# A norm moved between the weight pieces of a product, its factor in another buffer, and one attention unit held behind the query norms

## The chip, the core and the metric

The kernel runs on one core of a Trainium2 chip. The metric is the device time of one execution in microseconds (us); lower is better. The core has five engines that run side by side, each with its own queue of instructions in a fixed order: TensorE (PE in the profile, with its weight loads as PEld), VectorE (DVE), ScalarE (ACT), GpSimd (POOL) and SyncE (SP), which here issues most of the transfers.

## What is computed

One layer of a streaming encoder over 320 frames (256 of a prompt, 64 of a running stream), 2048 channels wide, all in float32:

```python
z = rmsnorm(x, ln_g) @ w_in                 # 1024 q, 128 k, 128 v, 1024 u, 1024 gate columns
q, k = rmsnorm(q, q_g), rmsnorm(k, k_g)     # per head of 64
attn_o = sink_attention(q, k_band, v_band, bias, sinks)
u, sv = gelu(zs)[..., :1024], rmsnorm(gelu(zs)[..., 1024:], g)
sgu_o = u * (ws @ sv + b_s)
mix = concatenate([rmsnorm(attn_o, g_a), rmsnorm(sgu_o, g_s)])
x = x + mix @ w_out
x = x + square(relu(rmsnorm(x, ln_ffn) @ w_up)) @ w_down
```

The norm of the attention output, `rmsnorm(attn_o, g_a)`, is the one that the change moves. As a norm's factor is one number per frame, the kernel multiplies by it behind the product: `g_a` goes into the left operand, the factor `rm_a` into the eviction of the W_out products.

## The kernel before

**Products.** Every large product is done by `products` (L115). It takes 256 output columns at a time and walks the contraction in weight pieces of 4 x 128 rows. Each piece is loaded by SP (`w_raw`, L103), split into a high and a low part (`w_hi` on ACT, L108; `w_lo` on DVE, L109), and multiplied with the high and low parts of the activations in 24 matmuls (L133). A product over 2048 channels has four pieces, 96 matmuls; a W_out product is one half of the contraction, two pieces, 48 matmuls. `w_hi` and `w_lo` have three buffers each, the accumulators in PSUM two. SP's loads are put in a fixed order by `issue_after` in `load`.

**Order.** A scheduler places each engine's instructions by a simulated timeline; it prefers what stands earlier in the program and pulls later work forward while that cannot run. Two tools hold it: `tc.issue_after(ins)` puts what is traced in its block behind `ins` on the same engine, and `between_pieces` of `products` puts a small piece of work behind weight piece number n of a product. In the second case the rest of the product stands behind `narrow[-1]`, the last matmul that the small work has recorded in the list `narrow`. Before the change, `rstd` (L163), `norm_q` (L306) and `values` (L318) record theirs there; `rstd_rows` (L152) and `spread` (L184) do not.

**First stage.** The first stage computes, in this order: keys, values and the first quarter of the queries; three more query products (q1 to q3), with the norms of earlier ones between their pieces; four gate products ("v", L465), among which ten attention units are spread (`attend_next` takes 4, 3, 3 and 0 units ahead of the four); four u products (L498); then 16 W_out products (L530), and the two MLP products. `norm_q(2)` stands behind piece 0 of q3; `norm_q(3)` behind q3.

**Attention units.** Unit n is one block of 64 frames and one of two key heads. Its score matmuls (L383) go into one PSUM tile `s_ps` (one buffer), DVE adds the bias with the query's norm `rq` (L392), maxima, exponentials (ACT, L407) and the division by the sum (POOL, L411) follow, then transposes (L421), their copy (L423), the product with the values (L427) and the copy into `ao` (L430).

**The norm of the attention output.** `add_square` sums the squares of `ao` in `acc_a` during u products 0 to 2 (POOL, L439). `rstd_rows` then takes the mean over the channels with six matmul instructions (three matmuls, L156, each of which the profile shows as two), an add on DVE (L158) and a power of -0.5 on POOL (L160); `spread` brings the result across all partitions with three more matmuls (L188, six in the profile) and copies it to `rm_a` (DVE, L190). Before, both stand behind the whole of the last u product (L511 to L513). `rm_a` is first used in the eviction of the first W_out product (L533).

**Memory.** `acc_a`, the bias, the gate's weights `wsT` and the gate's bias `sgb` lie in the pool `at`, which is closed behind the u products (L522). The pool `wf`, seven buffers for the weight pieces of W_out and of the MLP, is opened right behind it (L523) in the space that became free. The factors `rx`, `rk`, `rm_a`, `rm_s` and `r2` take turns in two buffers (`rstd_b`, L193); `rx` is read until the GELU of the last u product, `rk` until the keys are done.

Of the kernel before, what the change touches and what calls it, by code (L numbers as in the profile page):

```python
# [15 lines left out]
P = 128  # L16
# [4 lines left out]
KT = DM // P  # L21
DFF = 8192
FB = 16
EPS = 1e-6
# [6 lines left out]
def hymba_step_kernel(ctx: ExitStack, tc: tile.TileContext, i, o):  # L31
    nc = tc.nc
# [12 lines left out]
    def misc():  # L45
        return ps_m.tile([P, 512], F32, name="misc", tag="misc")
# [4 lines left out]
    def blk(name, shape, dt=F32):  # L51
        return actp.tile(shape, dt, name=name, tag="B", bufs=6)
# [15 lines left out]
    ident = const.tile([P, P], F32, name="ident")  # L68
# [10 lines left out]
    inv_1k = const.tile([P, 1], F32, name="inv_1k")  # L79
# [16 lines left out]
    loads, between, steps, narrow = [], [], [], []  # L96
# [18 lines left out]
    def products(w, k0, nk, c0, ps, rh, rl, deep=None, between_pieces={}):  # L115

        wv = w.rearrange("(kt p) n -> p kt n", p=P)
        behind = None  # L120
        steps.clear()
        for a in range(0, nk, 4):
            raw = (deep or wp).tile([P, 4, 256], F32, name="w_raw", tag="w_raw")
            hi, lo = w_tiles()
            load(raw, wv[:, k0 + a:k0 + a + 4, c0:c0 + 256])
            high, low = halves(raw, hi, lo)
            tail = isinstance(ps, list) and a + 4 == nk
            for k, g in [(k, g) for g in range(2) for k in range(4)] if tail else [(k, g) for k in range(4) for g in range(2)]:
                kk = a + k
                for x, (w_, r_) in enumerate(((hi, rh), (hi, rl), (lo, rh))):  # L130
                    out = ps[g][:, 0:T] if isinstance(ps, list) else ps[:, g, 0:T]
                    with tc.issue_after(behind) if behind else nullcontext():
                        mm = nc.tensor.matmul(out=out, lhsT=w_[:, k, g * P:(g + 1) * P], rhs=r_(kk),  # L133
                                              start=(kk == 0 and x == 0), stop=(kk == nk - 1 and x == 2))
            steps.append((high, low, mm.ins))
            if a // 4 in between_pieces:
                with tc.issue_after(mm.ins):
                    between_pieces[a // 4]()
                    behind = narrow[-1]

    def sums(name):
        return sm.tile([P, T], F32, name=name, tag="ssq", bufs=2)

    def acc_tile():
        return ps_acc.tile([P, 2, 512], F32, name="acc", tag="acc")

    def product(w, k0, nk, c0, rh, rl, deep=None, apart=False, **kw):
        ps = [misc(), misc()] if apart else acc_tile()
        products(w, k0, nk, c0, ps, rh, rl, deep=deep, **kw)
        return ps  # L150

    def rstd_rows(sq, weight, eps):  # L152

        st = misc()
        for t in range(3):
            nc.tensor.matmul(out=st[:, t:t + 1], lhsT=sq[:, t * P:(t + 1) * P], rhs=weight, start=True, stop=True)  # L156
        r = sm.tile([P, 3], F32, name="r_rows", tag="r_rows")
        nc.vector.tensor_scalar(out=r, in0=st[:, 0:3], scalar1=eps, scalar2=None, op0=ALU.add)  # L158
        rs = sm.tile([P, 3], F32, name="rs_rows", tag="rs_rows")
        nc.gpsimd.tensor_tensor(out=rs, in0=r, in1=nhalf[:, 0:3], op=ALU.pow)  # L160
        return rs
# [22 lines left out]
    def spread(rs, out):  # L184

        bc = misc()
        for t, (t0, n) in enumerate(TT):
            nc.tensor.matmul(out=bc[:, t0:t0 + n], lhsT=rs[:, t:t + 1].to_broadcast([P, P]),  # L188
                             rhs=ident[:, 0:n], start=True, stop=True)
        nc.vector.tensor_copy(out=out, in_=bc[:, 0:T])  # L190
        return out

    def rstd_b(name):  # L193
        return sm.tile([P, T], F32, name=name, tag="rstd_b", bufs=2)

    def split(src, g, hi, lo, pinned=False):

        pin = tc.keep_in_program_order if pinned else lambda ins: ins
        pin(nc.scalar.activation(out=hi, in_=src, func=AF.Copy, scale=g))
        pin(nc.vector.scalar_tensor_tensor(out=lo, in0=src, scalar=g, in1=hi.bitcast(F32), op0=ALU.mult,  # L200
                                           op1=ALU.subtract))
# [3 lines left out]
    xh, xl = (lambda k: XH[:, k]), (lambda k: XL[:, k])  # L205
    w_in = i["w_in"]
# [8 lines left out]
    for a, n in [(a, 1) for a in range(8)] + [(a, 2) for a in range(8, KT, 2)]:  # L215
# [16 lines left out]
        for x, (w_, r_) in enumerate(((hi, xh), (hi, xl), (lo, xh))):  # L232
            for j, k, g in [(j, k, g) for j in range(2) for k in range(n) for g in range(2)]:
                ps = q0_ps if j == 0 else kv_ps
                mm = nc.tensor.matmul(out=ps[:, g, 0:T], lhsT=w_[:, j, k, g * P:(g + 1) * P], rhs=r_(a + k),  # L235
                                      start=(a + k == 0 and x == 0), stop=(a + k == KT - 1 and x == 2))
# [46 lines left out]
    for k in range(0, KT, 2):  # L283
        sq = sm.tile([P, 2, T], F32, name="sq2", tag="w2", bufs=4) if k else ssq2
# [4 lines left out]
    ssq = sums("ssq")  # L289
    nc.vector.tensor_tensor(out=ssq, in0=ssq2[:, 0], in1=ssq2[:, 1], op=ALU.add)  # L290

    rx, rk = rstd_b("rx"), rstd_b("rk")

    rq = at.tile([P, 4, 10], F32, name="rq", bufs=1)

# [10 lines left out]
    def norm_q(g, sq):  # L306
        st = misc()
        for b in range(5):
            mm = nc.tensor.matmul(out=st[:, 2 * b:2 * b + 2], lhsT=sq[:, b].rearrange("p a t -> p (a t)"), rhs=hone,  # L309
                                  start=True, stop=True)  # L310
        narrow.append(mm.ins)
        r = at.tile([P, 10], F32, name="r_q", tag="r_q")
        nc.vector.tensor_scalar(out=r, in0=st[:, 0:10], scalar1=HD * EPS, scalar2=None, op0=ALU.add)
        nc.gpsimd.tensor_tensor(out=rq[:, g], in0=r, in1=nhalf[:, 0:10], op=ALU.pow)
# [26 lines left out]
    def keys():  # L341
        for dst, c in ((kn[:, 0:256], slice(0, 256)), (kn[:, 384:448], slice(256, 320))):
            nc.vector.scalar_tensor_tensor(out=dst, in0=zk[:, c], scalar=g_k, in1=rk[:, c], op0=ALU.mult, op1=ALU.mult)
        for h in range(2):
# [11 lines left out]
                    between_pieces={0: first_norms, 1: lambda: norm_q(1, q1_sq[0]), 2: keys})  # L356
# [76 lines left out]
    def add_square(acc, src, first):  # L433
        if first:
            nc.scalar.activation(out=acc[:, 0:T], in_=src, func=AF.Square)
        else:
            sq = sm.tile([P, T], F32, name="sq", tag="w1", bufs=3)
            nc.scalar.activation(out=sq, in_=src, func=AF.Square)
            nc.gpsimd.tensor_tensor(out=acc[:, 0:T], in0=acc[:, 0:T], in1=sq, op=ALU.add)  # L439

    todo = list(range(10))

    def attend_next(n):
        for _ in range(n):
            attend(todo.pop(0))


    def gelu2(ps, out):
# [10 lines left out]
    def sums_rows(name):  # L459
        t = at.tile([P, TP], F32, name=name, tag="ssq_rows", bufs=1)  # L460
        nc.gpsimd.memset(t[:, T:TP], 0.0)
        return t

    acc_v = sums_rows("acc_v")
    for g in range(4):  # L465
# [3 lines left out]
        for a in range(2 * g, 2 * g + 2):  # L469
            add_square(acc_v, gv[:, a], a == 0)  # L470
            nc.gpsimd.tensor_scalar(out=gv[:, a], in0=gv[:, a], scalar1=g_sv[:, a:a + 1], scalar2=None, op0=ALU.mult)
    nc.gpsimd.memset(wsT[HD:P, :, 0:HD], 0.0)
    rv = rstd_rows(acc_v, inv_1k, 4 * EPS)
    vnat = blk("vnat", [P, 2, 1024])
    vnat_s = at.tile([P, 1024], F32, name="vnat_s", bufs=1)
# [18 lines left out]
        nc.vector.tensor_tensor(out=gv[:, g, 256:T], in0=sp_ps[:, 256:T], in1=sgb[:, g, 0:HD], op=ALU.add)  # L494

    acc_s = sums("acc_s")
    SH = SL = None
    for g in range(4):  # L498
        u_ps = product(w_in, 0, KT, 1280 + g * 256, xh, xl)
        if g == 0:  # L500
            acc_a = sums_rows("acc_a")
            AH, AL = blk("AH", [P, 8, T], F32R), blk("AL", [P, 8, T], F32R)
            SH, SL = blk("SH", [P, 8, T], F32R), blk("SL", [P, 8, T], F32R)
        for x in range(2):
            a, (high, low, _) = 2 * g + x, steps[2 * x + 1]
            with tc.issue_after(high), tc.issue_after(low):
                split(ao[:, a], g_oa[:, a:a + 1], AH[:, a], AL[:, a])
        for x, a in enumerate(range(3 * g, min(3 * g + 3, 8))):
            with tc.issue_after(steps[x][0]):
                add_square(acc_a, ao[:, a], a == 0)  # L510
        if g == 3:  # L511
            with tc.issue_after(steps[0][0]), tc.issue_after(steps[0][1]):
                rm_a = spread(rstd_rows(acc_a, inv_1k, EPS), rstd_b("rm_a"))  # L513
        gu = sm.tile([P, 2, T], F32, name="gu", tag="w2", bufs=4)
        gelu2(u_ps, gu)
        sp = gv[:, 2 * g:2 * g + 2]
        nc.vector.scalar_tensor_tensor(out=sp, in0=sp, scalar=0.5, in1=gu, op0=ALU.mult, op1=ALU.mult)
        for a in range(2 * g, 2 * g + 2):
            add_square(acc_s, gv[:, a], a == 0)
            split(gv[:, a], g_os[:, a:a + 1], SH[:, a], SL[:, a])  # L520

# [6 lines left out]
    rm_s = rstd_b("rm_s")  # L528
    for half, (hi, lo, rm) in enumerate(((AH, AL, rm_a), (SH, SL, rm_s))):
        for g in range(8):  # L530
            ps = product(i["w_out"], 8 * half, 8, g * 256, lambda k: hi[:, k], lambda k: lo[:, k], wf)
            t = sm.tile([P, 2, T], F32, name="to", tag="w2", bufs=4)
# [15 lines left out]
    for b in range(nb):  # L548
        FH = [blk(f"FH{h}", [P, 8, T], F32R) for h in range(2)]
        FL = [blk(f"FL{h}", [P, 8, T], F32R) for h in range(2)]  # L550
        for g in range(FB // 2):
            ps = product(i["w_up"], 0, KT, (b * FB + 2 * g) * P, hh_, hl_, wf)
            t = sm.tile([P, 2, T], F32, name="tf", tag="w2", bufs=4)
# [83 lines left out]
```

## Time and profile before

| | |
|---|---|
| median of 3 timed runs | 1266.09 us (1265.51 to 1266.98) |
| the profiled execution: its time | 1261.78 us |
| its span, first to last instruction | 1259.8 us |
| mean granted clock of TensorE | 0.997 |
| DMA, mean over the span | 149 GB/s, 187.78 MB |
| HBM read / written | 182.91 MB / 3.32 MB |

A page of the profile gives busy times of the engines, the span in 40 slices, the DMA queues, the chain of work that ended last, and the costliest groups of instructions. Other views list who waited for whom, the busy time of each engine in a window, and the instructions in order of time. In the timeline a row has start, duration, engine, line of the code, operation, tiles as output<-inputs, shapes and count; a bracket at its end gives the idle time of the engine just ahead and what ended it. Matmuls overlap, so the distance between two starts, not the duration of one, is the pace. A trailing q in an engine's name (SPq) means its instruction queue. The columns of a window are length, busy time and instructions of PE, PEld, DVE, ACT and POOL, then the clock that TensorE was granted (1.00 is full), the share of the DMA engines, and GB/s.

### The profile page before, as it was taken

The page shows a single profiled execution, that of the slowest core. Times are in us where ns is not written, and L with a number is a line of the kernel's source. Part 1 is how long each engine was busy: PE and PEld are TensorE (multiplying, and loading weights), DVE is VectorE, ACT ScalarE, POOL GpSimd, SP SyncE. Part 2 cuts the span into 40 slices and gives each one's busy share as a digit, 9 for nine tenths or more (in the row PEclk, how much of TensorE's full clock was granted, in tenths as well). Part 3 has the DMA queues.
Part 4 walks back from the last instruction along what each step waited for, and adds up shares of the span by engine and source line. Part 5 has one row for each costly group of instructions (what it writes and reads, how often), then busy time and mean ns, then how long its engine had stood idle before and what let it go on. Part 6 is the DMA issues. An engine that isn't in the chain of part 4 may idle for free.

```text
span 1259.8 us, 20220 instructions
## 1 busy us (share of the span) xinstructions
PE 1248.1 (99%) x8519; PEld 1233.0 (98%) x8519; DVE 658.5 (52%) x767; ACT 489.7 (39%) x638; POOL 97.2 (8%) x97
## 2 busy tenths in 40 slices
PE   9999999899999999999999999999999999999998
PEld 8998899899999999999999999999999999999998
DVE  7857877676884444444444444444444334444443
ACT  7335555433543342223333333344333333343221
POOL 1223354200310000000000000000000000000000
PEclk9999999899999999999999999999999999999999
DMA  8643344554454444444454444445444454444550
GB/s 276 210 136 96 90 118 126 169 166 150 146 153 148 152 149 147 149 148 150 150 150 151 151 151 151 151 151 151 151 151 151 145 149 149 149 153 159 171 169 32
DMA packets 186555, 187.78 MB, mean 149 GB/s; under 512 B 6592, under 2 KB 185984, under 8 KB 186464
## 3 DMA queue, kind: packets, MB, share of 16 engines
q1 hardware_dynamic: 185824, 185.43, 47.4%
q8 instruction: 66, 1.08, 0.4%
q0 software_dynamic: 496, 1.03, 0.3%
q14 instruction: 25, 0.20, 0.0%
q10 hardware_dynamic: 144, 0.03, 0.0%
HBM read 182.91 MB, written 3.32 MB: 148 GB/s over the span
## 4 chain that ended last, share of the span: by engine, by line
PE 95%; DMA 2%; DVE 1%; SPq 1%; ACT 1%; issue 0%; ACTq 0%
PE acc L133 90%; PE misc L133 1%; DMA w_raw<-in_w_in 1%; SPq L103 1%; PE s_ps L383 1%; PE misc L427 1%; PE misc L421 1%; DMA b_dram<-b_row 1%; PE q_ps L235 0%; PE acc L235 0%; DMA w_first<-in_w_in 0%; PE misc L309 0%; ACT w_hi L108 0%; PE misc L489 0%; DMA w_raw<-in_w_out 0%
## 5 line engine op out<-in xcount | busy, mean ns | idle before, releaser
L109 DVE TENSOR_TENSOR w_lo<-w_raw,w_hi 128x1024 fp32r<-128x1024 f32 x332 | 414.0, 1247 | 438.6 <-ACT w_hi L108 430.1
L108 ACT ACTIVATE w_hi<-w_raw 128x1024 fp32r<-128x1024 f32 x332 | 351.5, 1059 | 685.5 <-PE acc L133 665.7
L133 PE MATMUL acc<-H2H,w_hi 128*128 128x320 f32 x1024 | 316.4, 309 | 0.0
L133 PE MATMUL acc<-H2L,w_hi 128*128 128x320 f32 x1024 | 316.4, 309 | 0.0
L133 PE MATMUL acc<-H2H,w_lo 128*128 128x320 f32 x1024 | 316.4, 309 | 0.0
L133 PE MATMUL acc<-FH,w_hi 128*128 128x320 f32 x992 | 306.5, 309 | 0.0
L133 PE MATMUL acc<-FL,w_hi 128*128 128x320 f32 x992 | 306.5, 309 | 0.0
L133 PE MATMUL acc<-FH,w_lo 128*128 128x320 f32 x992 | 306.5, 309 | 0.0
L133 PEld LDWEIGHTS acc<-H2L,w_hi 128*128 128x128 f32 x1024 | 192.2, 188 | 0.0
L133 PEld LDWEIGHTS acc<-H2H,w_hi 128*128 128x128 f32 x1024 | 192.2, 188 | 0.0
L133 PEld LDWEIGHTS acc<-H2H,w_lo 128*128 128x128 f32 x1024 | 192.2, 188 | 0.0
L133 PEld LDWEIGHTS acc<-FH,w_hi 128*128 128x128 f32 x992 | 186.2, 188 | 0.0
L133 PEld LDWEIGHTS acc<-FL,w_hi 128*128 128x128 f32 x992 | 186.2, 188 | 0.0
L133 PEld LDWEIGHTS acc<-FH,w_lo 128*128 128x128 f32 x992 | 186.2, 188 | 0.0
L133 PE MATMUL acc<-XH,w_hi 128*128 128x320 f32 x352 | 110.1, 313 | 0.1
L133 PE MATMUL acc<-XH,w_lo 128*128 128x320 f32 x352 | 110.0, 312 | 0.0
L133 PE MATMUL acc<-XL,w_hi 128*128 128x320 f32 x352 | 110.0, 312 | 0.0
L133 PEld LDWEIGHTS acc<-XH,w_hi 128*128 128x128 f32 x352 | 66.2, 188 | 1.6 <-issue 1.2
L133 PEld LDWEIGHTS acc<-XH,w_lo 128*128 128x128 f32 x352 | 66.1, 188 | 1.6 <-issue 1.4
L133 PEld LDWEIGHTS acc<-XL,w_hi 128*128 128x128 f32 x352 | 66.1, 188 | 1.2 <-issue 1.2
L554 DVE SCALAR_TENSOR_TENSOR tf<-acc,r 128x640 f32<-128x640 f32 x32 | 26.4, 825 | 41.9 <-PE acc L133 41.8
L568 DVE TENSOR_TENSOR xT<-xT,acc 128x640 f32<-128x640 f32 x31 | 25.5, 821 | 41.8 <-PE acc L133 41.8
(198 smaller groups left out, 1060.5 us busy)
## 6 DMA issues: line engine op xcount, KB each, us to landing
w_raw<-in_w_up SPq DMA_DIRECT2D x128, 512.0 KB
w_raw<-in_w_down SPq DMA_DIRECT2D x128, 512.0 KB
w_raw<-in_w_in SPq DMA_DIRECT2D x44, 512.0 KB
w_raw<-in_w_out SPq DMA_DIRECT2D x32, 512.0 KB
w_first<-in_w_in SPq DMA_DIRECT2D x15, 256.0 KB
out_yT<-xT SPq DMA_DIRECT2D x7, 320.0 KB
xT<-in_xT SPq DMA_DIRECT2D x8, 160.0 KB
xT<-in_xT SPq DMA_DIRECT2D x4, 320.0 KB
```

The costliest lines, as they stand in the source:

```text
L103: loads.append(nc.sync.dma_start(out=o_, in_=i_))
L108: return (pin(nc.scalar.activation(out=hi, in_=raw, func=AF.Copy)).ins, pin(nc.vector.tensor_tensor(out=lo, in0=raw, in1=hi.bitcast(F32), ...
L109: pin(nc.vector.tensor_tensor(out=lo, in0=raw, in1=hi.bitcast(F32), op=ALU.subtract)).ins)
L133: mm = nc.tensor.matmul(out=out, lhsT=w_[:, k, g * P:(g + 1) * P], rhs=r_(kk), start=(kk == 0 and x == 0), stop=(kk == nk - 1 and x == 2))
L383: nc.tensor.matmul(out=s_ps[:, p, j * nk:(j + 1) * nk], lhsT=qT[hs, blk_, a:a + 2].rearrange("p a t -> p (a t)"), rhs=kz[hs, kv, k0:k0 + n ...
L421: nc.tensor.transpose(out=pt_ps[0:n, (2 * p + j) * P:(2 * p + j + 1) * P], in_=s[:, p, j, c:c + n], identity=ident)
L427: nc.tensor.matmul(out=o_ps[p * HD:(p + 1) * HD, 0:256], lhsT=v[0:n, kv], rhs=pt[0:n, p * 256:(p + 1) * 256], start=(x == 0), stop=(x == l ...
L554: nc.vector.scalar_tensor_tensor(out=t, in0=ps[:, :, 0:T], scalar=0.0, in1=r2[:, None, :].to_broadcast([P, 2, T]), op0=ALU.max, op1=ALU.mult)
L568: nc.vector.tensor_tensor(out=xT[:, a:a + n], in0=xT[:, a:a + n], in1=p, op=ALU.add)
```

## The change

`rstd_rows` and `spread` record their last matmul in `narrow`, so that they can stand between the pieces of a product. In the last u product, the row norm of the attention output stands behind piece 0 and its spreading behind piece 2. `rk` is allocated ahead of `rx`, and `rm_a` ahead of the u products: it now follows `rk` in its buffer, where it followed `rx` before, and `rm_s` follows `rx`. The first attention unit's TensorE instructions stand behind the last matmul of `norm_q(3)`.

```diff
         st = misc()
         for t in range(3):
-            nc.tensor.matmul(out=st[:, t:t + 1], lhsT=sq[:, t * P:(t + 1) * P], rhs=weight, start=True, stop=True)
+            mm = nc.tensor.matmul(out=st[:, t:t + 1], lhsT=sq[:, t * P:(t + 1) * P], rhs=weight, start=True, stop=True)
+        narrow.append(mm.ins)
...
         for t, (t0, n) in enumerate(TT):
-            nc.tensor.matmul(out=bc[:, t0:t0 + n], lhsT=rs[:, t:t + 1].to_broadcast([P, P]),
-                             rhs=ident[:, 0:n], start=True, stop=True)
+            mm = nc.tensor.matmul(out=bc[:, t0:t0 + n], lhsT=rs[:, t:t + 1].to_broadcast([P, P]),
+                                  rhs=ident[:, 0:n], start=True, stop=True)
+        narrow.append(mm.ins)
...
-    rx, rk = rstd_b("rx"), rstd_b("rk")
+    rk, rx = rstd_b("rk"), rstd_b("rx")
...
     todo = list(range(10))
+    after_q = [narrow[-1]]
 
     def attend_next(n):
         for _ in range(n):
-            attend(todo.pop(0))
+            with tc.issue_after(after_q.pop()) if after_q else nullcontext():
+                attend(todo.pop(0))
...
     acc_s = sums("acc_s")
+    rs_a, rm_a = [], rstd_b("rm_a")
+    u_pieces = {3: {0: lambda: rs_a.append(rstd_rows(acc_a, inv_1k, EPS)), 2: lambda: spread(rs_a[0], rm_a)}}
     SH = SL = None
     for g in range(4):
-        u_ps = product(w_in, 0, KT, 1280 + g * 256, xh, xl)
+        u_ps = product(w_in, 0, KT, 1280 + g * 256, xh, xl, between_pieces=u_pieces.get(g, {}))
...
-        if g == 3:
-            with tc.issue_after(steps[0][0]), tc.issue_after(steps[0][1]):
-                rm_a = spread(rstd_rows(acc_a, inv_1k, EPS), rstd_b("rm_a"))
```

## The prediction

> **What bounds the kernel now.** I read the page's first part, then the windows, then the chain of waits around the one stretch where TensorE falls off.
>
> ```profile
> PE 1248.1 (99%) x8519; PEld 1233.0 (98%) x8519; DVE 658.5 (52%) x767; ACT 489.7 (39%) x638; POOL 97.2 (8%) x97
> 364.79 877.65 PE acc L133 x5984
> 230.00:235.00 5.00, 5.00 (x37) 4.92 (x35) 1.63 (x3) 0.00 (x0) 0.76 (x1) 1.00 0.00 0
> 235.00:240.00 5.00, 1.43 (x8) 1.24 (x7) 1.55 (x5) 2.01 (x3) 2.41 (x2) 0.67 0.73 242
> ```
>
> TensorE is busy 99% of the span, so only two things can change the time: stalls of TensorE, and matmuls that move between a stall and the dense stream. The long row of the chain gives the dense pitch: 877.65 / 5984 = 0.147 us per matmul. The windows (busy time of PE, PEld, DVE, ACT, POOL, then granted clock, DMA share, GB/s) show the deep hole: PE busy 1.43 of 5 us at clock 0.67. It lies between the last u product and the first W_out product. The DMA share just ahead of it is 0.00. The PE timeline and the chain through it:
>
> ```profile
> 234.14 0.31 PE L133 MATMUL acc<-XH,w_lo 128*128 128x320 f32 x1
> 234.28 0.72 PE L156 MATMUL misc<-inv_1k,acc_a 128*128 128x1 f32 x6
> 236.39 1.25 PE L188 MATMUL misc<-ident,rs_rows 128*128 128x128 f32 x6 [1.38 <-POOL rs_rows L160]
> 239.83 0.64 PE L133 MATMUL acc<-AH,w_hi 128*128 128x320 f32 x1 [2.19 <-ACT w_hi L108]
> ...
> 243.13 0.47 PE L133 MATMUL acc<-AH,w_hi 128*128 128x320 f32 x1
> 243.39 0.39 PE L133 MATMUL acc<-AL,w_hi 128*128 128x320 f32 x1
> 243.62 0.31 PE L133 MATMUL acc<-AH,w_lo 128*128 128x320 f32 x1
> SPq L103 <- PE misc L156: 17.3, 1, 17.3
> 235.09 3.53 DMA w_raw<-in_w_out
> 239.81 1.24 DVE w_lo L109
> ```
>
> The first W_out load waited 17.3 us on SP's queue for the L156 matmuls, the last readers of `acc_a`: the W_out buffers lie where that pool lay. So the norm of the attention output, put behind the whole last u product, holds back the load; load, halves and matmuls then follow one another (235.09 + 3.53, then w_hi, then w_lo to 241.05). From 234.28 to 243.62 PE started 11 W_out matmuls (from 239.83 on; 1.61 us at the dense pitch) in 9.34 us. **7.73 us** of this stretch is norm, waiting and slow clock.
>
> **Part 1: norm inside the last u product.** L156 moves behind weight piece 0, L188 behind piece 2. Nothing is removed; 12 PE instructions, one DVE add, one POOL power and one DVE copy move. Their PE price within a dense stream is read from the first norm (same shape as L156) and from the gate's matmuls (four with 128 columns, two with 64, the shapes of L188's six):
>
> ```profile
> 181.43 0.72 PE L156 MATMUL misc<-inv_1k,acc_v 128*128 128x1 f32 x6
> 182.01 0.63 PE L481 MATMUL misc<-ident,gv 128*128 128x128 f32 x4
> 213.39 0.60 PE L489 MATMUL misc<-wsT,vnat 128*128 128x128 f32 x4
> 213.83 0.33 PE L490 MATMUL misc<-wsT,vnat_s 128*128 128x64 f32 x2
> 213.97 0.39 PE L133 MATMUL acc<-XH,w_hi 128*128 128x320 f32 x1
> 214.20 0.30 PE L133 MATMUL acc<-XL,w_hi 128*128 128x320 f32 x1
> 216.87 2.22 POOL L439 TENSOR_TENSOR acc_a<-acc_a,sq 128x320 f32<-128x320 f32 x2
> 217.51 0.21 DVE L494 TENSOR_TENSOR gv<-misc,sgb 128x64 f32<-128x64 f32 x1
> ```
>
> L156: 182.01 - 181.43 = 0.58, plus 0.08 for the step back to the stream (213.97 to 214.20 is 0.23 instead of 0.147): 0.66. L188: 213.97 - 213.39 = 0.58, plus 0.08: 0.66. Together 1.32, so the part is worth 7.73 - 1.32 = **6.4 us**, if the other waits fall too. They should. The last u product is 96 matmuls, so it starts at 234.28 - 14.1 = 220.2 and piece 0 ends near 223.7. `acc_a` is complete at 219.09 (POOL, 216.87 + 2.22), 4.6 us ahead, so piece 1, now queued behind L156, does not wait. The load can go near 224.5 instead of 235.09. The other late readers of that pool, L490 (213.83) and L494 (217.51), are done. Its chain took 6.0 us (235.09 to 241.05), so the first halves could be ready near 230.5, 5 us ahead of need; the halves' buffers come free as u's pieces 1 and 2 end (about 228 and 231.5). DMA share in 230 to 235 was 0.00, so the transfer meets nothing. L188 comes about 7 us behind L156; the DVE add, POOL power and their hops took 2.1 us before (234.28 to 236.39), so piece 3 does not wait for L188 unless POOL or DVE is over 4 us late. The copy of the factor (L190) is first used by L533, behind the first W_out product (48 x 0.147 = 7 us). In rx's buffer the copy had to follow the last GELU's read of rx; in the keys' buffer it need not. I give the buffers nothing of their own (no reason for a gain or a loss: rk's last readers are the keys, whole products earlier, and rm_s, now in rx's buffer, is written in W_out, behind the last GELU).
>
> **Part 2: first attention unit behind the query norms.** Only TensorE instructions of unit 0 are held. Before, its score matmuls filled a hole ahead of the third query norm:
>
> ```profile
> 70.49 0.31 PE L133 MATMUL acc<-XH,w_lo 128*128 128x320 f32 x1
> 70.73 0.66 PE L383 MATMUL s_ps<-kzv,qT 64*128 64x64 f32 x6
> 72.48 0.44 PE L383 MATMUL s_ps<-kzv,qT 64*128 64x64 f32 x4 [1.10 <-DVE s L392]
> 72.85 1.28 PE L309 MATMUL misc<-hone,qsq 128*128 128x2 f32 x10
> 73.99 0.39 PE L133 MATMUL acc<-XH,w_hi 128*128 128x320 f32 x1
> 71.70 0.74 ACT L303 ACTIVATE qsq<-qT 128x640 f32<-128x640 f32 x1
> 88.30 0.31 PE L133 MATMUL acc<-XL,w_hi 128*128 128x320 f32 x1
> 88.54 0.44 PE L383 MATMUL s_ps<-kzv,qT 64*128 64x64 f32 x4
> 88.91 0.42 PE L133 MATMUL acc<-XH,w_lo 128*128 128x320 f32 x1
> 96.86 0.31 PE L133 MATMUL acc<-XL,w_hi 128*128 128x320 f32 x1
> 97.10 0.71 PE L383 MATMUL s_ps<-kzv,qT 64*128 64x128 f32 x8
> 97.74 0.41 PE L133 MATMUL acc<-XH,w_lo 128*128 128x320 f32 x1
> ```
>
> The hole is not unit 0's doing. The pieces of the fourth query product that are left stand behind norm_q(2) in the code, and that norm needs the eviction and the squares, which end at 72.44. Without the scores L309 starts at about 72.49, takes 1.14 (72.85 to 73.99), and the stream resumes at 73.63: 0.36 won. The 1.10 us wait thus goes, but the wait for the squares is late next. The scores of unit 0 and of unit 1 (which waits for the score buffer) then come in the dense stream: from matmul to matmul across them, less the pitch, plus 0.08 for the step back, eight cost 97.74 - 96.86 - 0.147 + 0.08 = 0.81, four cost 88.91 - 88.30 - 0.147 + 0.08 = 0.54. Two times eight in place of the four there now: 2 x 0.81 - 0.54 = 1.08 lost. Net **+0.7 us**. Bounds: -0.36 if the scores find another stall; +1.08 if L309 comes no earlier.
>
> What TensorE then shows between 70.7 and 72.5 is 1.8 us of unbroken idle. What that does to its clock no row shows; these windows are nearest. They are 3.41 us long because the low clock lasted twice that (236.73 to 243.56); the first lies around the same hole, the others around the drop:
>
> ```profile
> 69.47:72.89 3.41, 2.32 (x21) 1.92 (x19) 2.05 (x6) 1.74 (x2) 0.00 (x0) 1.00 0.53 158
> 233.31:236.73 3.41, 2.03 (x17) 1.95 (x16) 1.38 (x3) 0.74 (x1) 0.88 (x1) 1.00 0.12 34
> 236.73:240.14 3.41, 1.22 (x7) 1.03 (x6) 0.83 (x3) 1.42 (x2) 1.53 (x1) 0.50 0.99 334
> 240.14:243.56 3.41, 3.06 (x11) 2.66 (x11) 3.41 (x4) 1.98 (x3) 0.00 (x0) 0.50 1.02 326
> ```
>
> A stretch with PE busy 2.32 of 3.41 us kept clock 1.00; one with 2.03 ended in clock 0.50, and one busy stretch (3.06) at 0.50 ended that. The hole after the change would leave about 3.41 - 1.75 = 1.66 busy: below the one that dropped. The price is one such stretch at half clock: matmuls went at 0.26 (243.13 to 243.39), so 3.41 x (1 - 0.147 / 0.26) = **1.5 us**. Ends: 0 and 1.5; I take 1.5, since 1.66 is nearer to 2.03 than to 2.32. [...]
>
> **Sum.** 1259.8 - 6.4 + 0.7 + 1.5 = 1255.6 us of span, 4.2 less. The profiled run took 1261.78, 2.0 more than its span; the timed median, 1266.09, lies 4.3 above that run. I carry the difference over: 1266.09 - 4.2 = **1261.9 us**.
>
> **Rivals.** (a) The clock holds in the hole: 1266.09 - 6.4 + 0.7 = 1260.4. For it: the same hole kept 1.00 with 1.10 us of idle. Against: the row of 2.03. [...]
> (b) Attention, begun later, falls against a full DVE, and w_lo or the copies of probabilities come late:
>
> ```profile
> 115.00:120.00 5.00, 5.00 (x37) 4.01 (x36) 5.00 (x11) 2.06 (x8) 3.40 (x3) 1.00 0.39 118
> PE misc L421 <- ACT ao L430: 0.7, 2, 0.4
> ```
>
> DVE was busy 5.00 of 5 us there. Two more waits like the two of 0.7 in all, and one more half-clock stretch: +0.7 + 1.5 gives 1261.9 + 2.2 = 1264.1, within a measurement of no change. Against: the v and u products fill TensorE whatever attention does, and unit 1 waited for the fourth norm already.
> (c) The load isn't freed: something else of the old pool, or a neighbour in SP's order, is read until the end of u. Then 7.73 stays (the moved norm hides in the wait), part 2 remains: 1266.09 + 0.7 + 1.5 = 1268.3, slower. It decides from the point where the load goes later than about 229.6 (u's end, now 234.28 + 1.32 = 235.6, less 6.0). Against: SP's one long wait names L156 alone.
>
> **Chances.** Forecast 0.50, (a) 0.30, (b) 0.14, (c) 0.06. About 0.2% (2.5 us) is what a measurement can tell from no change, so faster ends at 1263.6. Forecast and (a) stand below it but for a tail, (b) in it, (c) above: faster 0.78, same 0.16, slower 0.06. The range takes in (a) with part 2's lower bound (1260.4 - 1.1 = 1259.3, and 0.3 for prices) and (b): 1259.0 to 1264.5.
>
> **What would show it.** L156 near 224 and L188 near 231 inside the last u product; the first W_out load near 224.5; PE busy 5.00 and clock 1.00 from 235 to 245. At 70 to 74: idle before L309 of some 1.8 us, released by the squares, no score matmuls until the fourth norm, and clock 0.5 for 3.4 us behind it. Wrong would be: a load that waits for another releaser, PE waiting for rs_rows or `acc_a` in the last u product, or new idle time between 90 and 180.

## The result, and the profile after

In the first comparison the changed kernel took **1256.57 us** (median of 4, 1254.9 to 1257.21) and the kernel before, beside it, 1265.8 us (median of 4): ratio 0.9929, 95% interval 0.9917 to 0.9941, so 9.2 us faster. The forecast was 1261.9 us and its range began at 1259.0: the direction was right, the gain more than twice the forecast one. Repeated later, the changed kernel took 1257.17 us against 1264.78: ratio 0.9949 (0.9937 to 0.9961), 7.6 us by the medians. The first comparison lies at the wide end.

The page of the changed kernel, its first rows (busy time, share of the span, instructions). Lines of code stand up to three further down than before: L309 is now L311, L188 is L189.

```profile
span 1253.1 us, 20226 instructions
PE 1245.4 (99%) x8519; PEld 1231.4 (98%) x8519; DVE 658.8 (53%) x767; ACT 490.8 (39%) x638; POOL 97.0 (8%) x97
```

The work is the same (8519 TensorE instructions both times); TensorE was busy 2.7 us less and the span fell from 1259.8 to 1253.1. The windows over the place of the old deep hole, with PE, PEld, DVE, ACT, POOL, clock, DMA share and GB/s:

```profile
230.00:235.00 5.00, 5.00 (x37) 5.00 (x36) 3.89 (x5) 1.58 (x3) 1.93 (x2) 1.00 1.06 349
235.00:240.00 5.00, 5.00 (x37) 5.00 (x36) 2.45 (x3) 2.77 (x4) 1.58 (x1) 1.00 1.08 343
```

PE 5.00 at clock 1.00 stands where 1.43 at 0.67 stood, and the DMA share in the first window is 1.06 where it was 0.00. The chain of waits through it (start, duration, engine, line), then the row of SP's waits, then the row of SP's timeline with the first W_out load, all of the changed kernel:

```profile
217.99 5.57 PE acc L133 x38
223.56 0.56 PE misc L156 x6
224.12 7.15 PE acc L133 x48
231.27 0.61 PE misc L189 x6
231.89 13.26 PE acc L133 x90
```

```profile
SPq L103 <- PE misc L156: 6.3, 1, 6.3
```

```profile
224.21 25.07 SPq L103 DMA_DIRECT2D w_raw<-in_w_out  x13
```

The chain never leaves TensorE: norm, spreading and W_out follow one another without a wait. The load goes at 224.21 instead of 235.09 and SP waits 6.3 us for L156 instead of 17.3. The hole ahead of the third query norm, in the PE timeline of the changed kernel, and in its windows:

```profile
70.72 0.31 PE L133 MATMUL acc<-XH,w_lo 128*128 128x320 f32 x1
72.72 1.28 PE L311 MATMUL misc<-hone,qsq 128*128 128x2 f32 x10 [1.69 <-ACT qsq L305]
73.85 0.40 PE L133 MATMUL acc<-XH,w_hi 128*128 128x320 f32 x1
```

```profile
69.25:72.67 3.42, 1.78 (x13) 1.51 (x11) 1.66 (x3) 1.74 (x2) 0.00 (x0) 1.00 0.65 176
72.67:76.08 3.41, 3.37 (x25) 3.37 (x26) 0.73 (x2) 0.00 (x0) 1.73 (x1) 1.00 0.45 124
```

The scores have left the hole, and the idle time of 1.69 us ends with the squares, as forecast. But the clock stayed at 1.00 with PE busy 1.78 of 3.42 us, where I had put a half-clock stretch.

### The profile page after: what moved, and what is told of

It reads as the page before. It is cut to its first block, busy times and chain, and to the rows that moved or that the text cites. A ratio compares the mean times of both kernels' runs of the same rounds, so it can differ in the third digit from the quotient of the medians.

```text
span 1253.1 us, 20226 instructions
## 1 busy us (share of the span) xinstructions
PE 1245.4 (99%) x8519; PEld 1231.4 (98%) x8519; DVE 658.8 (53%) x767; ACT 490.8 (39%) x638; POOL 97.0 (8%) x97
## 3 DMA queue, kind: packets, MB, share of 16 engines
q8 instruction: 66, 1.08, 0.4%
## 4 chain that ended last, share of the span: by engine, by line
PE 96%; DMA 2%; SPq 1%; ACT 0%; DVE 0%; issue 0%; ACTq 0%
PE acc L133 91%; PE misc L133 1%; DMA w_raw<-in_w_in 1%; PE misc L429 1%; PE s_ps L385 1%; DMA b_dram<-b_row 1%; PE misc L423 1%; SPq L103 1%; PE q_ps L237 0%; PE acc L237 0%; PE misc L311 0%; DMA w_first<-in_w_in 0%; ACT w_hi L108 0%; PE misc L493 0%; PE misc L485 0%; DVE w_lo L109 0%
```

## The experiments

Two questions were open: which part brings the gain, and what the clock has to do with it. Each comparison is with the kernel before, run beside it on the same chip; gains are differences of medians unless a ratio is named.

**The kernel before, once more** (no edit).

> The kernel before, unchanged, so that its executions can be seen one by one. The change gained 9.2 us in the timed runs and 6.7 us between the two profiled spans. Theory A (granted clock): the profiled execution of before, span 1259.8 at clock 0.997, was one of the shortest; in most executions TensorE gets half clock for longer around the two holes, so spans lie near 1263 to 1264 with clock 0.995 or 0.996, and the times 2 us above the spans, at 1265 to 1266. Theory B (something outside the span, or another chip): spans near 1259.8 at clock 0.997, the times 6 us above them.

Measured: 1265.49 us (12 runs, 1263.3 to 1268.26), ratio 1.0004 (0.9993 to 1.0015). Its profiled execution had a span of 1266.3 us at a mean clock of 0.993, where the one of the prediction had 1259.8: the same program differs by 6.5 us. Two windows of this trace around each of two places:

```profile
49.20:52.62 3.42, 1.51 (x10) 1.54 (x11) 3.42 (x6) 2.02 (x4) 1.13 (x2) 1.00 0.32 92
52.62:56.04 3.42, 3.42 (x15) 3.42 (x14) 1.34 (x2) 0.39 (x2) 0.00 (x0) 0.50 0.59 181
73.11:76.52 3.41, 2.31 (x21) 1.91 (x19) 2.44 (x6) 1.74 (x2) 0.00 (x0) 1.00 0.58 154
76.52:79.93 3.41, 3.41 (x16) 3.41 (x16) 1.10 (x7) 1.53 (x9) 1.61 (x1) 0.50 0.52 149
79.93:83.34 3.41, 3.41 (x14) 3.41 (x14) 0.32 (x2) 0.00 (x0) 0.98 (x2) 0.50 0.03 12
```

So the kernel before has half-clock stretches outside the deep hole too. The second place is the same query hole, with the scores still in it: 2.31 of 3.41 us busy, then 0.50 for two stretches. In the trace that I predicted from, 2.32 busy was followed by 1.00. Its waits show where the first place comes from (waiting instruction, releaser, us in all, times, longest):

```profile
PE acc L133 <- ACT ksq L332: 2.0, 1, 2.0
```

By the chains of the traces, a load of `w_in` that SP issues behind the gate's tables lands more or less late: at 46.05 us in the trace of the prediction, at 46.58 in the first of the changed kernel, at 47.74 here. The wait that TensorE then has for the squares of the keys (`ksq`) is 0.1, 0.4 and 2.0 us.

How usual is that? A stretch of 3.41 us at half clock takes 0.5 x 3.41 / 1260 = 0.0014 off the mean clock. The deep hole's two stretches alone give 0.997. Of 52 executions of the kernel before (these 12, and 40 that ran beside the experiments down to the filled deep hole), 16 show 0.997, 27 show 0.996 (one stretch more), and 9 show 0.993 to 0.995 (two or three more): about 0.9 more on the average, counted so. The prediction's trace, with none more, is one of the shorter ones.

**Each part alone.** The norm without the held unit (the changed kernel less the order), and the held unit without the norm (the kernel before plus that order):

```diff
-    after_q = [narrow[-1]]
...
-            with tc.issue_after(after_q.pop()) if after_q else nullcontext():
-                attend(todo.pop(0))
+            attend(todo.pop(0))
```

> The norm between the pieces and the buffer of the keys, without the order on the first attention unit. Theory A: the freed W_out load is nearly all of the gain; the order on unit 0 gave 0.9 us in the profiled span, so 1257 to 1258. Rival C (the prediction's own step): the order on unit 0 costs 0.7 us and 1.5 us of clock, so without it 1254 to 1255.

> Only the order on the first attention unit; the norm stays behind the last u product. Theory A: within 1.5 us of before (the hole ahead of the third query norm becomes 1.7 us of unbroken idle and in most executions costs one half-clock stretch, against 0.9 us won in attention), 1264.5 to 1266.5. Rival C: 2.2 us slower than before, 1268.

Measured: the norm alone 1258.67 us (6 runs), ratio 0.9946 (0.9929 to 0.9963), which is 6.8 us of 1264.58. The unit alone 1264.04 us (12 runs), ratio 0.9994 (0.9983 to 1.0005), 0.8 us, not told from nothing. What follows: the norm carries nearly all of it, and the unit costs nothing where I had +0.7, and +1.5 more for the clock. The mean clocks of the unit alone say the same: four of its twelve executions show 0.997, five 0.996 and three 0.995, about 0.9 stretches beyond the deep hole, as in the kernel before. The norm alone shows nine stretches in six executions. The windows of the norm alone:

```profile
70.31:73.72 3.41, 2.31 (x21) 1.91 (x19) 2.40 (x6) 1.74 (x2) 0.00 (x0) 1.00 0.51 155
73.72:77.13 3.41, 3.41 (x15) 3.41 (x16) 1.13 (x6) 1.50 (x9) 1.52 (x1) 0.50 0.51 145
77.13:80.54 3.41, 3.41 (x14) 3.41 (x14) 0.34 (x2) 0.03 (x1) 1.07 (x2) 0.50 0.05 16
```

With the scores in the hole, the clock falls here too, and for two stretches. Without them the hole of the changed kernel lost no clock in its first profile. So "less busy in the hole, therefore slower" is not what decides from execution to execution.

**The third query norm one piece later** (the changed kernel): does the hole matter, if the pieces of q3 can run first?

```diff
-    q3_ps = product(w_in, 0, KT, 768, xh, xl, between_pieces={0: lambda: norm_q(2, q2_sq)})
+    q3_ps = product(w_in, 0, KT, 768, xh, xl, between_pieces={1: lambda: norm_q(2, q2_sq)})
```

> The changed kernel with norm_q(2) behind piece 1 of the fourth query product instead of piece 0, so that piece 1 fills the hole while the squares are made. Theory A: the idle 1.7 us goes and so does the half-clock stretch there: clock 1.000 in all executions, time 1252.5 to 1253.5, 3 to 4 us below the changed kernel. Rival D (the low clock of the changed kernel's longer executions, 0.999, comes from another place): 1.7 us less, 1254.9, with clock 0.999 as before.

Measured: 1257.07 us (6 runs, 1255.71 to 1262.52), ratio 0.9945 (0.9926 to 0.9964): no different from the changed kernel. The PE timeline of this kernel shows why it tells little:

```profile
74.81 0.31 PE L133 MATMUL acc<-XH,w_lo 128*128 128x320 f32 x1
76.48 0.42 PE L133 MATMUL acc<-XH,w_hi 128*128 128x320 f32 x1 [1.36 <-ACT w_hi L108]
77.11 1.35 PE L311 MATMUL misc<-hone,qsq 128*128 128x2 f32 x10
```

The wait for the squares went, and a wait of 1.36 us for a weight half took its place. That is a miss: neither the gain nor the full clock that was expected, and nothing decided about the hole.

**The changed kernel again, its hole filled, and its tables loaded later.** Seven matmuls of the identity keep TensorE busy in the hole; their result is not used. Separately, the loads of the gate's bias and weights move to behind the q2 product in the code; in the trace SP issues them from 48.62 us on, where the changed kernel did from 38.08.

```diff
+    with tc.issue_after(steps[-1][2]):
+        fill_ps = misc()
+        for _ in range(7):
+            nc.tensor.matmul(out=fill_ps[:, 0:P], lhsT=ident, rhs=ident, start=True, stop=True)
     q2_sq = evict_q(2, q2_ps)
```

```diff
-    between.append((sgb.rearrange("p g i -> p (g i)"), i["sgu_b"].to_broadcast([P, 1024])))
-    between.append((wsT, i["sgu_wT"]))
...
+    between.append((sgb.rearrange("p g i -> p (g i)"), i["sgu_b"].to_broadcast([P, 1024])))
+    between.append((wsT, i["sgu_wT"]))
     q2_sq = evict_q(2, q2_ps)
```

> The changed kernel, unchanged, in more executions. So far before had 35 executions with a median near 1264.7 and spans from 1259.5 to 1266.3, by their clock (0.993 to 0.997) and by a late weight load near 49 us. Theory A (the parts add: 6.4 us from the freed load, some 0.9 from attention's waits, and the half-clock stretches of the first hole are paid in both kernels): median 1256.5 to 1257.5, ratio 0.993 to 0.9945. Theory E (the prediction's sum, 4.2 us): 1260.5.

> The changed kernel with seven matmuls of the identity on itself, into a PSUM tile that nobody reads, behind the third query product, so that TensorE is busy in the 1.7 us in which it waits for the squares. Nothing else moves. Theory A (that hole is what puts TensorE at half clock in most executions): clock 1.000 in nearly all, median 1.0 to 1.5 us below the changed kernel. Rival D (the clock falls elsewhere, as behind the late load at 49 us): clock 0.999 or lower as often as without, no gain.

> The changed kernel with the two tables of the gate (sgb, wsT; 0.5 MB each) loaded behind the third query product's loads instead of ahead of a weight piece at 39 us; TensorE's order is the same. Theory F (these 1 MB make the load behind them late by up to 2 us in some executions, which also costs clock): no wait for the squares of the keys near 49 us, scatter of the spans halved, median 1 to 1.5 us below the changed kernel. Rival G (the lateness comes from the bias rows' small packets or from the memory): no change within 0.5 us.

Measured: the changed kernel 1257.17 us (5 runs), mean clock 1.000 in one, 0.999 in three, 0.997 in one. Filled: 1255.44 (6 runs), ratio 0.9934 (0.9921 to 0.9946), clock 1.000 in five of six. Tables later: 1255.46 (5 runs), ratio 0.9931 (0.9919 to 0.9943), clock 0.999 in four of five. Each brings 1.7 us by the medians, though the intervals overlap with the changed kernel's. The PE timeline of the filled hole:

```profile
70.88 0.31 PE L133 MATMUL acc<-XH,w_lo 128*128 128x320 f32 x1
71.02 1.72 PE L363 MATMUL misc<-ident 128*128 128x128 f32 x14
72.87 1.28 PE L311 MATMUL misc<-hone,qsq 128*128 128x2 f32 x10
74.01 0.39 PE L133 MATMUL acc<-XH,w_hi 128*128 128x320 f32 x1
```

The norm and the stream come no earlier from the last matmul on (3.13 us, unfilled 73.85 - 70.72 = 3.13), so what the fill brings is clock: by the mean clocks one stretch in six executions, where the changed kernel has eight in nine, some 1.1 us of the 1.7 at the price worked out below. The kernel with later tables has no wait at 49 us at all. Its scatter, which was to be halved, is not smaller (1253.71 to 1256.79 us, the changed kernel beside it 1256.9 to 1259.62). Its profile has the half-clock stretch that the prediction had expected of the changed kernel:

```profile
69.55:72.96 3.41, 1.73 (x15) 1.46 (x13) 2.05 (x2) 1.74 (x2) 0.00 (x0) 1.00 0.48 154
72.96:76.37 3.41, 3.41 (x15) 3.41 (x15) 0.17 (x1) 0.00 (x0) 1.98 (x1) 0.50 0.55 158
76.37:79.78 3.41, 3.41 (x25) 3.41 (x24) 0.27 (x1) 1.06 (x1) 0.00 (x0) 1.00 0.01 3
```

By the starts of the same large matmuls in the two traces, that stretch cost 1.56 us against the first profile of the changed kernel. The forecast price of 1.5 is right; whether it is paid differs between executions: 1.73 busy here, 1.78 there.

**Is the old deep hole's loss the clock?** The kernel before, with identity matmuls in the two waits of that hole (6 behind L156, 9 behind L188), at full clock but with the late load:

```diff
-                rm_a = spread(rstd_rows(acc_a, inv_1k, EPS), rstd_b("rm_a"))
+                rs_a = rstd_rows(acc_a, inv_1k, EPS)
+                fill(narrow[-1], 6)
+                rm_a = spread(rs_a, rstd_b("rm_a"))
+                fill(narrow[-1], 9)
```

> The kernel before with matmuls of the identity in its deep hole (6 between the norm's row sums and its spreading, 9 behind it), so that the clock is kept while the wait for the W_out load stays. Theory A (of the 7.7 us that the hole costs, 3.9 us are waits, 1.3 the norm itself, some 2.5 half clock): clock 0.998 or 0.999 instead of 0.996, median 2 to 2.5 us below before, that is 1262 to 1262.7, so most of the change's gain is left. Rival H (the clock is the main part): 4 us or more below before.

Measured: 1263.22 us (11 runs), ratio 0.9987 (0.9978 to 0.9995), so 1.6 us gained, somewhat less than the 2 to 2.5 that I expected; the middle one of the mean clocks goes up from 0.996 to 0.998. In its trace, at a mean clock of 1.000, the way from the last matmul of u to the 48th of W_out takes 13.44 us, in the trace of the prediction 14.76, so 1.3 us less. The changed kernel takes 7.04, with its norm 1.33 us more (both worked out below), so 5.1 us of the hole stay at full clock. The clock of the deep hole, which this takes away, is a small part of what the change gains; most is the late load itself. Its PE timeline: the fill ends, and the weight halves are still waited for.

```profile
238.32 2.23 PE L199 MATMUL misc<-ident 128*128 128x128 f32 x18
240.84 0.41 PE L133 MATMUL acc<-AH,w_hi 128*128 128x320 f32 x1 [0.29 <-ACT w_hi L108]
242.10 0.41 PE L133 MATMUL acc<-AH,w_lo 128*128 128x320 f32 x1 [0.70 <-DVE w_lo L109]
```

**The load's release as a dose.** The changed kernel with the row norm two pieces later and the spreading one later:

```diff
-    u_pieces = {3: {0: lambda: rs_a.append(rstd_rows(acc_a, inv_1k, EPS)), 2: lambda: spread(rs_a[0], rm_a)}}
+    u_pieces = {3: {2: lambda: rs_a.append(rstd_rows(acc_a, inv_1k, EPS)), 3: lambda: spread(rs_a[0], rm_a)}}
```

**The buffer.** The changed kernel with `rx` allocated ahead of `rk` again:

```diff
-    rk, rx = rstd_b("rk"), rstd_b("rx")
+    rx, rk = rstd_b("rx"), rstd_b("rk")
```

**Filled hole and later tables together**, the version that the runs so far pointed to.

> The changed kernel with the norm's row sums behind piece 2 of the last u product and its spreading behind piece 3, so that the first W_out load goes 7 us later, at about 231.8 on the clock of the changed kernel's profile. Theory A (the W_out chain of load and halves, 6.0 us, decides, and the load follows the row sums): the halves are ready at about 237.8, TensorE waits some 2 us from 235.3 on, and it may lose a half-clock stretch (1.5 us): 1259 to 1261. Rival J (the gain came from taking the norm out of the way, not from the load): within 0.5 us of the changed kernel.

> The changed kernel with the factor in the buffer of rx again (rx allocated ahead of rk), the norm still between the pieces. Prediction's step (the buffer is worth nothing of its own on TensorE's path): as the changed kernel, 1256.5 to 1257.5. Rival I (the copy has to follow the last GELU's read of rx, and what waits for it comes late): 1 us or more slower.

> The changed kernel with both additions at once: the gate's tables loaded later and the identity matmuls in the hole of the third query norm. Theory A and F together: no wait near 49 us, clock 1.000 in every execution, spans within 1.5 us of each other near 1252.5, median 1254, below the changed kernel (1257.2) and either addition alone (1255.4).

Measured, all in one session (kernel before 1264.36 us): rows later 1260.48 us (5 runs), ratio 0.9967 (0.9955 to 0.998); `rx` first 1257.04 (5 runs, 1254.37 to 1257.57), ratio 0.9936 (0.9924 to 0.9949); filled hole and later tables **1254.67** (5 runs, 1254.06 to 1255.43), ratio 0.992 (0.9906 to 0.9933), clock 1.000 in all five.

The chain of the kernel with the later rows:

```profile
235.18 0.57 PE misc L156 x6
235.82 3.61 DMA w_raw<-in_w_out
239.53 1.07 ACT w_hi L108
240.68 1.24 DVE w_lo L109
```

Behind L156 the chain leaves TensorE for the load, and comes back by w_hi and w_lo: the path of the old hole, shorter. TensorE's timeline of the same kernel has the two waits:

```profile
240.65 0.42 PE L133 MATMUL acc<-AH,w_hi 128*128 128x320 f32 x1 [0.66 <-ACT w_hi L108]
241.96 0.41 PE L133 MATMUL acc<-AH,w_lo 128*128 128x320 f32 x1 [0.75 <-DVE w_lo L109]
```

By the starts of the same matmuls, the move puts W_out 1.89 us further back against the changed kernel's trace; by the medians it costs 3.4 us against 1257.04, and the rest of that is not accounted for. The query hole of this trace, empty of scores as in the changed kernel, was followed by two half-clock stretches. They lie ahead of the moved norm and are not in the 1.89:

```profile
71.10:74.52 3.42, 1.74 (x13) 1.47 (x12) 1.88 (x2) 1.74 (x2) 0.00 (x0) 1.00 0.56 166
74.52:77.93 3.41, 3.41 (x16) 3.41 (x16) 0.33 (x2) 0.00 (x0) 1.41 (x1) 0.50 0.54 159
77.93:81.34 3.41, 3.41 (x15) 3.41 (x14) 0.00 (x0) 0.00 (x0) 0.58 (x1) 0.50 0.01 2
```

The loss returns as the release moves later, with the same two norm pieces in the same product: the release of the load is what part 1 is worth.

With `rx` first nothing changes in the time. Two rows of its DVE timeline:

```profile
231.65 0.48 DVE L192 COPY rm_a<-misc 128x320 f32<-128x320 f32 x1
234.80 0.82 DVE L454 TENSOR_TENSOR z<-acc,rx 128x640 f32<-128x640 f32 x1 [1.55 <-PE acc L133]
```

The factor is written 3 us ahead of the last GELU's read of `rx`, so it does not lie in that buffer even with this order of allocation: the edit did not make the case that it was meant to make, and shows only that the order of the two names is worth nothing. It also leaves open whether `rm_a` followed `rx` in the kernel before, where `rx` was allocated first as well.

The kernel with the filled hole and the later tables has the lowest median measured, 2.4 us below 1257.04, though the two intervals still overlap (to 0.9933, from 0.9924). It is 0.7 us above the 1254 that I expected. All five of its executions lie within 1.4 us; the five with `rx` first spread over 3.2, the nine of the kernel before beside them over 2.4.

## Why the prediction was wrong

**What held.** What bounds the kernel, the mechanism of part 1, and its size against the trace that I summed from. The PE timeline of the changed kernel at the three places of the last u product:

```profile
223.26 0.31 PE L133 MATMUL acc<-XH,w_lo 128*128 128x320 f32 x1
223.40 0.72 PE L156 MATMUL misc<-inv_1k,acc_a 128*128 128x1 f32 x6
223.99 0.39 PE L133 MATMUL acc<-XH,w_hi 128*128 128x320 f32 x1
...
231.11 0.78 PE L189 MATMUL misc<-ident,rs_rows 128*128 128x128 f32 x6
231.69 0.39 PE L133 MATMUL acc<-XH,w_hi 128*128 128x320 f32 x1
...
235.15 0.31 PE L133 MATMUL acc<-XH,w_lo 128*128 128x320 f32 x1
235.30 0.31 PE L133 MATMUL acc<-AH,w_hi 128*128 128x320 f32 x1
```

L156 takes 223.99 - 223.40 = 0.59 and L189 0.58 us of the stream; with the 0.08 of each step back, 1.33, where 1.32 was forecast. The last matmul of u stands at 235.15, before at 234.14: 1.01 later, so the trace had been 0.32 ahead where u began. The twelfth W_out matmul starts at 235.30 + 11 x 0.147 = 236.92 instead of 243.62: 6.70 earlier, of which 0.32 was there already. Against this trace part 1 is worth **6.4 us, as forecast**. The forecast signs came: L156 near 224, L189 near 231, the load at 224.21 (forecast 224.5), full windows from 235 to 245, no wait for `acc_a` or `rs_rows`. The norm alone, 6.8 us by its ratio (4.7 to 9.0), agrees. Rival (c), a load that isn't freed, falls.

But that trace had the cheapest deep hole of three. From the start of the last matmul of u to that of the 48th of W_out it takes 14.76 us there (234.14 to 248.90), 15.26 in the kernel before once more (240.13 to 255.39), 16.05 in the unit alone (235.01 to 251.06), and 7.04 in the changed kernel (235.15 to 242.19). All three have 6.83 us at half clock, which begin 2.6, 3.6 and 5.4 us behind the last matmul of u, so that less or more of the dense stream falls into them. Less the 7.04 and the 1.33, the hole is worth 6.4, 6.9 and 7.7 us, 7.0 on the average: some 0.6 of the miss is the size of this term, taken from one draw.

**The step that failed: the clock term, +1.5 us.** I charged a half-clock stretch in the hole to the changed kernel and none to the kernel before, because the trace that I summed against had none there. The price was right for one stretch (1.56), though behind the later rows' query hole two came (3.12). The difference was not: the kernel before pays such a stretch in most executions, 0.9 beyond the deep hole on the average. The changed kernel pays as many: of nine executions (the first comparison and the repeat) two show a mean clock of 1.000, six 0.999 and one 0.997, together eight stretches, or 0.9 each. The unit alone, whose query hole is that of the changed kernel, has 0.9 beyond the deep hole too. The term is about 0. My comparison of 1.66 busy with a row that kept the clock (2.32) and one that lost it (2.03) took two single stretches for a threshold; 2.31 lost it in two later traces, and 1.78 kept it. The half-clock stretches of the traces, 3.41 us or twice that long, begin 0.38, 0.43 and 0.94 us behind the first matmul of the query norm (73.72, 76.52 and 72.96 in the traces of the norm alone, the kernel before once more and the later tables), and executions of one kernel differ in their mean clock (0.997 to 1.000 in the changed kernel, 0.993 to 0.997 in the kernel before). So whether a stretch is paid differs from execution to execution in both kernels, and I had treated it as fixed by the change. With the term at 0, rival (a)'s sum of 1260.4 comes out, though not by its mechanism: the clock doesn't always hold in the hole.

**Part 2, +0.7 us, was wrong in its sign by the traces.** I compared the starts of the same large matmuls in the traces of the changed kernel and of the kernel before, from just ahead of the hole to the start of the last u product: the difference goes from +0.53 to -0.32, 0.85 us won. The kernel with the unit alone, against the same trace, also wins 0.85 there. The hole itself gives 0.67 (0.36 forecast; two of the scores that had also stood ahead of the hole, among transposes, went too, some 0.3). The moved scores should then have cost 1.08 in the dense stream. In place of a loss the rest, up to the last u product, brings about 0.2 more. In the trace of the kernel before, the waits from 90 to 180 us were the two of 0.7 that the prediction shows and one more:

```profile
PE misc L427 <- DVE pt L423: 0.3, 1, 0.3
```

The norm alone still has both groups in the same stretch:

```profile
PE misc L423 <- ACT ao L432: 0.7, 2, 0.4
PE misc L429 <- DVE pt L425: 0.3, 1, 0.3
```

The changed kernel and the unit alone have neither row: 1.0 us of waits that the held unit takes away, which about pays for the scores. I had asked only whether it would bring new waits (rival b), and none came, so that rival falls. Why the two groups go when unit 0 is issued later is seen, not taken apart. The whole of part 2 is below what the comparison of the unit alone can tell from nothing (0.8 us; -2.1 to +0.6), but the 2.2 us that I had added for the unit and its clock together lie outside that interval.

**Carrying over.** I put the difference of a profiled execution onto a median, after writing that the median stood 4.3 us above that execution. That is allowed only if what makes up the 4.3 is the same in both kernels; I had summed a stretch for one side from its hole, and for the other from a single draw, and the deep hole from that draw too.

**The buffers** were given nothing, and the time is the same in both orders. My reason, that in the buffer of `rx` the copy had to follow the last GELU, was not tested, since the factor doesn't lie there in either case.

**The sum as measured**: -7.0 for the norm (-6.4 against the prediction's trace), -0.85 for the unit, 0 for the clock, together some -7.9 us. The repeat gave 7.6 by the medians, and 6.5 by its ratio (4.9 to 8.0); the session with `rx` first, the same time in effect, 7.3 by the medians. The first comparison's 9.2 (7.5 to 10.5 by its interval) holds 1.3 us more than the sum; I have only the scatter of the kernel before to put it down to, of which four executions stood there. Against the forecast gain of 4.2 the sum is 3.65 larger: 1.5 is the clock term, 1.55 part 2 and 0.6 the deep hole.

**What stays open**: what decides whether a thinly used stretch is followed by half clock. Neither the busy time in it nor its longest idle gap sorts the traces here; the last section has the rows. Also open is why the held unit takes the two groups of waits away.

## What to carry to other kernels

Look at what the last reader of a buffer holds back, not only at what it costs: six narrow matmuls in front of a load were worth 6.4 us and more, and two pieces of a product later a part of that was lost again. Before a rare event (a half-clock stretch, a late load) is charged to the changed kernel, ask how often the kernel before already pays for it; one profiled execution doesn't say, a row of mean clocks over many does. Where such an event scatters between executions, closing its cause may be worth an edit of its own: a later table load and a few dummy matmuls in a known hole brought 2.4 us here by the medians, with intervals that overlap.

## What the runs showed of the hardware

The clock fell behind stretches in which TensorE was busy for most of the time: in two traces with the scores in the hole (the kernel before once more, the norm alone) its longest idle gap was 1.1 us, 2.31 of 3.41 us were busy, and 0.50 followed for 6.83 us. Another execution (the changed kernel's) with a gap of 1.69 us and 1.78 busy kept 1.00.

The busy time of the 3.41 us around this hole does not sort its traces. With the scores, 2.32 kept 1.00 (the prediction's trace) and 2.31 lost it (the two above). Without them, 1.78 and 1.94 kept it (the changed kernel; its repeat, 70.71 to 74.12), less than the 2.31 that lost it, and 1.73 and 1.74 lost it (tables later, rows later). Near 49 us the kernel before once more lost it behind 1.51 busy. What decides is not shown by any run here.

Nor does the busy time of a half-clock stretch say whether a second follows. TensorE was busy for all 3.41 us of the first one in four traces of this hole: three had a second behind it (the norm alone, the kernel before once more, rows later), one went back to 1.00 (tables later). The scores in the hole do not decide it, as the hole of the later rows had none and lost two.
